# An encoder layer with 32 experts on one core: the block between the experts' weight products in another order

## The chip, the cores and the metric

One core of one Trainium2 chip runs the whole layer in one launch. The metric is the device time of the launch in microseconds (us), median of several runs. The kernel before takes 993.62 us (3 runs, 993.09 to 994.04).

## What is computed

The layer has three parts on 512 tokens of 1024 channels: a mixer (convolution and dilated attention), a cross-attention into 256 memory rows, and a mixture of 32 SwiGLU experts of width 512 with two experts per token; a last RMSNorm follows. The change lies in the experts and the last norm:

```
gates = p_g[:, None] * softmax(top_v)                # two experts per token
y_rows = (silu(xb @ w1[e]) * (xb @ w3[e])) @ w2[e]   # for the tokens of expert e
y = segment_sum(y_rows * row_gate, row_tok)          # back to the tokens
out = rms_norm(x + y, final_norm_g)
```

Every expert's weights (6.29 MB in float32) are read once: 201 MB in all.

## The kernel before

Each expert has 64 slots; two experts are a pair, whose 2 x 64 slots fill the 128 rows of a tile. `RK` holds for each token and expert the rank of the token in the expert (0 if it isn't there), `RT` is its transpose in bf16, experts on the partitions. `experts` (L1213) runs eight **rounds** d = 0 to 7 of four experts (two pairs):

- **Products.** `experts_up` multiplies the gathered tokens `xT` by w1 and w3 of the four experts of round d (PSUM banks "pj" for the first pair, "s" for the second). From round 1 on, `experts_down` then multiplies the hidden rows of round d-1, `eT`, by w2 (banks "tr","tr" for the first pair, "o","m" for the second) and `gated` scales the result by the slots' gates: ScalarE writes the high part of `ys`, VectorE the low part.
- **The block between.** `hidden_turned` turns the new hidden rows (8 transposes, "pj"). `hot` writes the one-hot matrix `onehot` of the next four experts (VectorE), `gather4` gathers their tokens by 64 matmuls of 128x256 (`onehot` against the rows `hm`; banks "s","s","pj","pj"), and `put` copies them to `xT`. `one_hots` makes `ct`, the transposed one-hots of round d-1's experts: for each of the four experts a matmul that spreads one row of `RT` over 128 partitions of a "tr" bank, and a compare on VectorE of 64 of these partitions with the slot number. `slot_gates` computes the gates of the next slots (8 matmuls of 128x8 into "o" and "m", read by ScalarE and VectorE). `scatter` adds the outputs to the tokens: 8 tiles of four matmuls 128x512 (`ct` against `ys`; banks "tr","o","tr","m"), each followed by an add to `xacc` on VectorE (L1211).

Round 0 has no down products and no scatter, round 7 no gather. Behind the loop stand the last round's two pairs: pair 14 (`one_hots`, `experts_down`, `scatter`) and pair 15 (`experts_last`: three groups of columns, each with its product, `gated` and `scatter`, and the last norm's steps between). `finish_begin` (L1279) prepares the last norm: it spreads `final_norm_g` over 128 partitions, `fg`, with eight VectorE products, eight matmuls (L1292, 16 in the trace) and two ScalarE copies (L1293); `fg` is first read by GpSimd at L1305, behind the scatter of the first group.

TensorE's instructions inside the rounds are kept in the order in which the code is written; the other engines' order is set when the program is built, by a scheduler.

**Weights.** They come in pieces of 512 KB, 48 in a full round, over SyncE's queue, into a ring of 29 regions in SBUF. A piece is issued when the products have read the region's former content (`load` at the end of each step of the products), at most eight are under way, and they are issued in the order of use. So the transfers run ahead of the products by up to 29 pieces.

Of the kernel before, what the change touches and what calls it, by code (L numbers as in the profile page):

```python
# [12 lines left out]
AF = mybir.ActivationFunctionType  # L13
ALU = mybir.AluOpType
# [4 lines left out]
D = 1024  # L19
# [8 lines left out]
NE = 32  # L28
# [9 lines left out]
V_XA, V_MEM, V_MOE, V_DW, V_DB, V_LG, V_LB, V_CO, V_AO, V_FN, V_MIX, V_N = 0, 8, 16, 24, 86, 88, 90, 92, 94, 100, 108, 116  # L38
# [31 lines left out]
def rows(ap, n):  # L70

    return bass.AP(tensor=ap.tensor, offset=ap.offset, ap=[[0, 128], [1, n]])
# [12 lines left out]
class K:  # L85
# [984 lines left out]
            return oh, x, rest  # L1070
        return add, end

    def gather4(self, d, oh, xT):

        for b, tag in enumerate(("s", "s", "pj", "pj")):
            p = self.ps(tag)
            for cc in (2 * b, 2 * b + 1):
                for t in range(NT):
                    self.take(p, oh, cc, t, t == 0, t == NT - 1)
            for cc in (2 * b, 2 * b + 1):  # L1080
                self.put(xT, p, cc)
# [28 lines left out]
                self.nc.vector.tensor_tensor(gt[q, j:j + 1], gt[q, j:j + 1], p[q, 4 + e:5 + e], op=ALU.add)  # L1110
        return gt

    def one_hots(self, pr, ct):

        for i in range(2):
            p = self.ps("tr")
            e = 2 * pr + i
            self.mm(p, self.idb[:, e:e + 1].to_broadcast([128, 128]), self.RT, start=True, stop=True)
            q = slice(i * 64, i * 64 + 64)
            self.nc.vector.tensor_scalar(ct[q, :], p[q, :], self.slot[q, :], None, op0=ALU.is_equal)  # L1120

    def experts_up(self, d, xT, rest=None):

# [34 lines left out]
    def hidden(self, j):  # L1158
        return self.eT[:, j, :].rearrange("p (a b) -> p a b", a=4)

    def experts_down(self, pr, gt):

        j = pr % 2
        hT = self.hidden(j)
        ps = [self.ps(tag) for tag in (("tr", "tr"), ("o", "m"))[j]]
        for k in range(4):
            w = [self.piece(pr, 2, k, e) for e in range(2)]
            for h in range(2):
                for i in range(2):
                    self.mm(ps[h][i * 64:i * 64 + 64, :], hT[:, k, i * 64:i * 64 + 64], w[i][:, h, :],  # L1170
                            start=k == 0, stop=k == 3)
            self.load(2)
        out = []
        for h in range(2):
            ys = self.wsp.tile([128, 2, 512], F32R, name="ys", tag="wlo")
            self.gated(ys, ps[h], gt, 512)
            out.append(ys)
        return out
# [34 lines left out]
    def experts(self, oh, xT, rest):  # L1213


        self.sl = self.eT = None
        with self.in_order():
            gt, ys = None, []
            for d in range(NE // 4):
                self.experts_up(d, xT, rest if d == 0 else None)  # L1220
                last = d == NE // 4 - 1
                if d == 0:
                    now = self.slot_gates(0, oh)
                if d:
                    ys = [self.experts_down(2 * d - 2 + j, gt[:, j:j + 1]) for j in range(2)]
                gt = now
                self.hidden_turned()
                if not last:
                    for t in range(NT):
                        self.hot(oh, d + 1, t)  # L1230
                    self.gather4(d + 1, oh, xT)
                if d:
                    ct = self.wsp.tile([128, 2, 512], F32R, name="ct", tag="whi")
                    for j in range(2):
                        self.one_hots(2 * d - 2 + j, ct[:, j, :])
                if not last:
                    now = self.slot_gates(d + 1, oh)
                if d:
                    for h in range(2):
                        self.scatter([(ct[:, j, :], ys[j][h]) for j in range(2)], h * 512, 512, ("tr", "o", "tr", "m"))  # L1240
                    ys = ct = None
            xT = None
            ct = self.wsp.tile([128, 2, 512], F32R, name="ct", tag="whi")
            for j in range(2):
                self.one_hots(NE // 2 - 2 + j, ct[:, j, :])
            y = self.experts_down(NE // 2 - 2, gt[:, 0:1])
            for h in range(2):
                self.scatter([(ct[:, 0, :], y[h])], h * 512, 512, ("tr", "o", "tr", "m"))
        self.experts_last(NE // 2 - 1, self.hidden(1), ct[:, 1, :], gt[:, 1:2])
# [29 lines left out]
    def finish_begin(self):  # L1279

        nc = self.nc
        r = [self.region(PIECES.index((NE // 2 - 3, 2, k, e))) for k in range(4) for e in range(2)]
        flat = [v.rearrange("p a b -> p (a b)") for v in r[0:6]]
        self.fg, dg, self.fo = flat[0], flat[1], flat[2:6]
        self.fj, self.fk = r[6][:, 0, :], r[6][:, 1, :]
        for i in range(2):
            p = self.ps("pj")
            for c in range(4):
                d = dg[:, i * 512 + c * 128:i * 512 + c * 128 + 128]
                v = V_FN + i * 4 + c  # L1290
                nc.vector.tensor_scalar(d, self.ident, self.VT[:, v:v + 1], None, op0=ALU.mult)
                nc.tensor.matmul(p[:, c * 128:c * 128 + 128], self.ones, d, start=True, stop=True)  # L1292
            nc.scalar.activation(self.fg[:, i * 512:i * 512 + 512], p, AF.Copy)  # L1293
        self.fss = self.xm.tile([128, NT, 3], F32, name="fss")
        self.frs = self.sm.tile([128, NT], F32, name="frs", bufs=1)

# [284 lines left out]
```

## Time and profile before

| what | value |
|---|---|
| median of 3 runs | 993.62 us |
| the profiled execution's own time | 992.92 us |
| its span, first to last instruction | 991.1 us |
| TensorE matmul busy | 954.9 us (96%) |
| VectorE busy | 465.6 us (47%) |
| ScalarE busy | 304.3 us (31%) |
| HBM read | 239.96 MB |

The profile's times are us from the start of the span. A matmul's end is modelled, so durations of neighbouring matmuls overlap; the distance from one start to the next is what counts. A float32 product of 128x512 appears as two instructions. The granted clock is a share of 2.4 GHz: 1.00 is 2.4 GHz, 0.50 is 1.2 GHz.

### The profile page before, as it was taken

Reading aid. Unit: us, or ns where it says so; the run is one execution under the profiler, and the core shown is the slowest. Engines: PE = TensorE matmul, PEld = TensorE weight load, DVE = VectorE, ACT = ScalarE, POOL = GpSimd, SP = SyncE. Lnnn points to the kernel's source line nnn. Section 1 sums busy time; section 2 is a strip of 40 time slices with the busy share of each in tenths; the row PEclk is TensorE's granted clock in tenths of the full one; section 3 lists DMA queues with packets and bytes.
Section 4 is the critical chain, followed back from the end, with each engine's and each line's share of the span. In section 5 each row is a group of like instructions: output and inputs, shape, how many; then the busy total and the mean of one; then the engine's idle time right before and its main releaser. Section 6 shows DMA issues by size and latency. Waiting matters only on the chain.

```text
span 991.1 us, 15255 instructions
## 1 busy us (share of the span) xinstructions
PE 954.9 (96%) x5804; PEld 652.3 (66%) x5804; DVE 465.6 (47%) x1110; ACT 304.3 (31%) x683; POOL 202.0 (20%) x245
## 2 busy tenths in 40 slices
PE   8999999999999999999999899899899999999994
PEld 7988788878899988999363543735436345364352
DVE  6679777777756455547220420502414124032256
ACT  7525565656534445435110200101011010020113
POOL 3159998973310001101000000000000000000002
PEclk9999999999999999999999989899998998999997
DMA  6421201222364126653889999999999999999932
GB/s 214 135 80 48 81 29 38 64 87 85 120 219 142 44 86 234 255 191 128 324 326 397 409 341 409 409 353 409 382 409 409 377 409 364 400 409 400 404 104 87
DMA packets 102744, 243.10 MB, mean 245 GB/s; under 512 B 11288, under 2 KB 51596, under 8 KB 102668
## 3 DMA queue, kind: packets, MB, share of 16 engines
q1 hardware_dynamic: 102668, 242.09, 65.2%
q8 instruction: 47, 0.77, 0.3%
q14 instruction: 29, 0.24, 0.1%
HBM read 239.96 MB, written 2.10 MB: 244 GB/s over the span
## 4 chain that ended last, share of the span: by engine, by line
PE 89%; DVE 6%; POOL 2%; issue 1%; DMA 1%; SPq 0%; ACT 0%; DVEq 0%; POOLq 0%; ACTq 0%
PE ps_pj L147 36%; PE ps_s L147 21%; PE ps_tr L147 9%; PE ps_o L147 6%; PE ps_m L147 6%; PE ps_o L587 2%; PE ps_tr L573 2%; PE ps_s L552 2%; DVE ct L1120 1%; PE ps_s L551 1%; PE ps_pj L151 1%; POOL sg L424 1%; DVE onehot L1027 1%; PE ps_tr L151 1%; DVE xacc L1211 1%
## 5 line engine op out<-in xcount | busy, mean ns | idle before, releaser
L147 PE MATMUL ps_pj<-ring,xT 128*64 128x512 f32 x504 | 111.8, 594 | 0.3 <-DVE xT L1043 0.3
L147 PE MATMUL ps_s<-ring,xT 128*64 128x512 f32 x496 | 107.8, 592 | 0.0
L1305 POOL TENSOR_TENSOR ring<-xacc,ring 128x512 f32<-128x512 f32 x4 | 5.0, 1284 | 503.0 <-DVE xacc L1211 503.0
L115 DVE TENSOR_TENSOR wlo<-wst,whi 128x512 fp32r<-128x512 f32 x104 | 79.7, 797 | 30.2 <-ACT whi L114 29.7
L147 PEld LDWEIGHTS ps_s<-ring,xT 128*64 128x64 f32 x496 | 35.6, 137 | 70.8 <-issue 65.9
L147 PEld LDWEIGHTS ps_pj<-ring,xT 128*64 128x64 f32 x504 | 36.0, 137 | 70.1 <-issue 66.7
L114 ACT ACTIVATE whi<-wst 128x512 fp32r<-128x512 f32 x108 | 62.4, 625 | 47.8 <-PE ps_pj L147 14.0
L147 PE MATMUL ps_pj<-whi,hT_hi 128*128 128x256 f32 x256 | 74.9, 293 | 0.3 <-DVE rv L502 0.3
L147 PE MATMUL ps_pj<-wlo,hT_hi 128*128 128x256 f32 x256 | 74.5, 292 | 0.0
L147 PE MATMUL ps_pj<-whi,hT_lo 128*128 128x256 f32 x256 | 73.6, 288 | 0.0
L147 PE MATMUL ps_tr<-ring,eT 128*64 128x512 f32 x256 | 56.5, 593 | 0.0
L1145 DVE TENSOR_TENSOR sl<-sl,ps_s 128x512 f32<-128x512 f32 x8 | 5.5, 688 | 103.9 <-PE ps_s L147 103.9
L1145 DVE TENSOR_TENSOR sl<-sl,ps_pj 128x512 f32<-128x512 f32 x8 | 5.5, 689 | 102.8 <-PE ps_pj L147 92.1
L147 PEld LDWEIGHTS ps_pj<-whi,hT_hi 128*128 128x128 f32 x256 | 48.8, 191 | 4.3 <-issue 3.1
L147 PEld LDWEIGHTS ps_pj<-wlo,hT_hi 128*128 128x128 f32 x256 | 48.8, 191 | 2.4 <-issue 2.2
L147 PEld LDWEIGHTS ps_pj<-whi,hT_lo 128*128 128x128 f32 x256 | 48.9, 191 | 1.7 <-issue 1.7
L1144 ACT ACTIVATE sl<-ps_pj 128x512 f32<-128x512 f32 x8 | 4.8, 597 | 146.8 <-PE ps_pj L147 146.8
L560 ACT ACTIVATE pw<-pw,nm 128x512 f32<-128x512 f32 x48 | 34.5, 719 | 31.6 <-DVE nm L558 28.0
L147 PEld LDWEIGHTS ps_tr<-ring,eT 128*64 128x64 f32 x256 | 18.3, 137 | 36.2 <-issue 36.0
L424 POOL TENSOR_TENSOR sg<-sg,ctmp 128x512 f32<-128x512 f32 x30 | 41.4, 1378 | 1.3
L563 POOL TENSOR_SCALAR pw<-pw,rd 128x512 f32<-128x512 f32 x48 | 37.1, 775 | 21.3 <-DVE rd L562 14.2
L147 PE MATMUL ps_tr<-ys,ct 128*128 128x512 f32 x120 | 40.2, 460 | 0.5 <-DVE ct L1120 0.5
(386 smaller groups left out, 2134.7 us busy)
## 6 DMA issues: line engine op xcount, KB each, us to landing
ring<-in_w_dram SPq DMA_DIRECT2D x374, 512.0 KB
wst<-in_w_in_dram SPq DMA_DIRECT2D x24, 256.0 KB
wst<-in_w_in_dram SPq DMA_DIRECT2D x10, 512.0 KB
wst<-in_w_xk_dram SPq DMA_DIRECT2D x8, 512.0 KB
wst<-in_w_xv_dram SPq DMA_DIRECT2D x8, 512.0 KB
wst<-in_w_out_dram SPq DMA_DIRECT2D x8, 512.0 KB
wst<-in_w_xq_dram SPq DMA_DIRECT2D x8, 512.0 KB
wst<-in_w_xo_dram SPq DMA_DIRECT2D x8, 512.0 KB
```

Source lines behind the costliest of these rows:

```text
L114: nc.scalar.activation(hi, src, AF.Copy)
L115: (eng or nc.vector).tensor_tensor(lo, src, hi.bitcast(F32), op=ALU.subtract)
L147: ins = self.nc.tensor.matmul(*args, **kw)
L151: ins = self.nc.tensor.transpose(out, in_, self.ident)
L424: nc.gpsimd.tensor_tensor(self.cacc[:, 0, :], self.cacc[:, 0, :], tmp, op=ALU.add)
L551: nc.tensor.matmul(p, q, kh, start=True, stop=False)
L552: nc.tensor.matmul(p, q[own, :], kl[own, :], start=False, stop=True)
L560: nc.scalar.activation(w, w, AF.Exp, bias=nm, scale=0.125, accum_out=den)
L563: nc.gpsimd.tensor_scalar(w, w, rd, 1.0, op0=ALU.mult, op1=ALU.mult)
L573: self.nc.tensor.transpose(p2[:, kt * 128:kt * 128 + 128], ws[t][:, kt * 128:kt * 128 + 128], self.ident)
L587: nc.tensor.matmul(o[i * 64:i * 64 + 64, half * 256:half * 256 + 256], v[kt][:, vo + i * 64:vo + i * 64 + 64], pts[i][half][:, kt, :], sta ...
L1145: nc.vector.tensor_tensor(sl, sl, hs[1], op=ALU.mult)
```

## The change

`ranks_spread` is new: it spreads the ranks of two experts into one bank, 64 partitions each, so that `one_hots` compares 128 partitions at once (two compares a round and not four). The spreads stand right behind the down products, the compares ahead of the gather on VectorE, the gates between the two halves of the gather. Behind the loop, pair 14's spreads stand ahead of its product, which now goes into the banks "s","s". `final_norm_g` comes to 128 partitions by one DMA.

```diff
-    def gather4(self, d, oh, xT):
+    def gather4(self, d, oh, xT, tags):
-        for b, tag in enumerate(("s", "s", "pj", "pj")):
+        for b, tag in tags:
...
-    def one_hots(self, pr, ct):
+    def ranks_spread(self, pr):
+        p = self.ps("tr")
         for i in range(2):
-            p = self.ps("tr")
             e = 2 * pr + i
-            self.mm(p, self.idb[:, e:e + 1].to_broadcast([128, 128]), self.RT, start=True, stop=True)
-            q = slice(i * 64, i * 64 + 64)
-            self.nc.vector.tensor_scalar(ct[q, :], p[q, :], self.slot[q, :], None, op0=ALU.is_equal)
+            self.mm(p[i * 64:i * 64 + 64, :], self.idb[:, e:e + 1].to_broadcast([128, 64]), self.RT, start=True, stop=True)
+        return p
+
+    def one_hots(self, p, ct):
+        self.nc.vector.tensor_scalar(ct, p, self.slot, None, op0=ALU.is_equal)
...
-                if d:
-                    ys = [self.experts_down(2 * d - 2 + j, gt[:, j:j + 1]) for j in range(2)]
-                gt = now
-                self.hidden_turned()
                 if not last:
                     for t in range(NT):
                         self.hot(oh, d + 1, t)
-                    self.gather4(d + 1, oh, xT)
+                if d:
+                    ys = [self.experts_down(2 * d - 2 + j, gt[:, j:j + 1]) for j in range(2)]
+                    spread = [self.ranks_spread(2 * d - 2 + j) for j in range(2)]
+                gt = now
+                self.hidden_turned()
                 if d:
                     ct = self.wsp.tile([128, 2, 512], F32R, name="ct", tag="whi")
                     for j in range(2):
-                        self.one_hots(2 * d - 2 + j, ct[:, j, :])
+                        self.one_hots(spread[j], ct[:, j, :])
                 if not last:
+                    self.gather4(d + 1, oh, xT, ((0, "s"), (1, "s")))
                     now = self.slot_gates(d + 1, oh)
+                    self.gather4(d + 1, oh, xT, ((2, "pj"), (3, "pj")))
...
+            spread = [self.ranks_spread(NE // 2 - 2 + j) for j in range(2)]
+            y = self.experts_down(NE // 2 - 2, gt[:, 0:1], ("s", "s"))
             ct = self.wsp.tile([128, 2, 512], F32R, name="ct", tag="whi")
             for j in range(2):
-                self.one_hots(NE // 2 - 2 + j, ct[:, j, :])
-            y = self.experts_down(NE // 2 - 2, gt[:, 0:1])
+                self.one_hots(spread[j], ct[:, j, :])
...
-        for i in range(2):
-            p = self.ps("pj")
-            for c in range(4):
-                ...
-                nc.vector.tensor_scalar(d, self.ident, self.VT[:, v:v + 1], None, op0=ALU.mult)
-                nc.tensor.matmul(p[:, c * 128:c * 128 + 128], self.ones, d, start=True, stop=True)
-            nc.scalar.activation(self.fg[:, i * 512:i * 512 + 512], p, AF.Copy)
+        nc.sync.dma_start(self.fg, rows(self.a["final_norm_g"], D))
```

How the instructions move. TensorE in the block of a middle round, before (`ps_tr<-rkT,idb` is a spread, `early,sl` the transposes, `onehot,hm` the gather, `ghl,onehot` the gates, `ys,ct` the scatter; the spread stands four times in a row):

```order
L151 MATMUL ps_pj<-early,sl 128x128 x8
L147 MATMUL ps_s<-onehot,hm 128x256 x32
L147 MATMUL ps_pj<-onehot,hm 128x256 x32
L147 LDWEIGHTS idb
L147 MATMUL ps_tr<-rkT,idb 128x512
...
L147 MATMUL ps_o<-ghl,onehot 128x8 x4
L147 MATMUL ps_m<-ghl,onehot 128x8 x4
L147 MATMUL ps_tr<-ys,ct 128x512 x4
```

The same place in the changed kernel:

```order
L147 LDWEIGHTS idb
L147 MATMUL ps_tr<-rkT,idb 64x512
...
L151 MATMUL ps_pj<-early,sl 128x128 x8
L147 MATMUL ps_s<-onehot,hm 128x256 x32
L147 MATMUL ps_o<-ghl,onehot 128x8 x4
L147 MATMUL ps_m<-ghl,onehot 128x8 x4
L147 MATMUL ps_pj<-onehot,hm 128x256 x32
L147 MATMUL ps_tr<-ys,ct 128x512 x4
```

The spreads went from between gather and scatter to ahead of the transposes, and the gates from just ahead of the scatter to the middle of the gather; nothing but gather matmuls stands ahead of the scatter now.

VectorE in the same block of the changed kernel (`ys` is the gating, `ct` the compare, `xT` the copy of gathered tokens, `gt` the gates, L1027 the one-hots of the round after next):

```order
L1188 SCALAR_TENSOR_TENSOR ys<-ps_m,gt,ys 128x512
L108 COPY eT<-ps_pj 128x512
L1123 TENSOR_SCALAR ct<-ps_tr,early 128x512 x2
L1043 TENSOR_SCALAR xT<-ps_s,gmo 128x256 x2
L1110 TENSOR_TENSOR gt<-gt,ps_o 64x1
L1110 TENSOR_TENSOR gt<-gt,ps_m 64x1
...
L1043 TENSOR_SCALAR xT<-ps_pj,gmo 128x256 x2
L1027 TENSOR_TENSOR onehot<-iota,RK 128x256 x4
L1214 TENSOR_TENSOR xacc<-xacc,ps_tr 128x512
```

The compares are ahead of every copy of the gather. The four one-hots L1027 stand whole ahead of the first add of the scatter.

TensorE behind the loop, from the last tile of round 7's scatter, before (`ring,eT` into "tr" is pair 14's product, into "s" pair 15's):

```order
L147 MATMUL ps_tr<-rkT,idb 128x512
L147 MATMUL ps_s<-ring,eT 64x512 x2
...
L147 MATMUL ps_tr<-ring,eT 64x512 x14
L147 MATMUL ps_s<-ring,eT 64x512 x2
L147 MATMUL ps_s<-ring,eT 64x256 x8
L147 MATMUL ps_tr<-ys,ct 128x512 x2
L147 MATMUL ps_o<-ys,ct 128x512 x2
```

The same place in the changed kernel:

```order
L147 MATMUL ps_tr<-rkT,idb 64x512
L147 MATMUL ps_s<-ring,eT 64x512 x16
L147 MATMUL ps_tr<-ys,ct 128x512 x2
L147 MATMUL ps_o<-ys,ct 128x512 x2
...
L147 MATMUL ps_s<-ring,eT 64x512 x8
L147 MATMUL ps_s<-ring,eT 64x256 x8
L147 MATMUL ps_o<-y_8733,ct 128x512 x2
```

Pair 15's first product was spread between pair 14's spreads and product; now it stands behind pair 14's whole scatter.

## Rows read from the trace of the kernel before

**Rows 1.** The page: the engines' busy time (us, share of the span, instructions), and what the DMA engines moved in each of 40 slices of 24.8 us, in GB/s.

```profile
PE 954.9 (96%) x5804; PEld 652.3 (66%) x5804; DVE 465.6 (47%) x1110; ACT 304.3 (31%) x683; POOL 202.0 (20%) x245
...
GB/s 214 135 80 48 81 29 38 64 87 85 120 219 142 44 86 234 255 191 128 324 326 397 409 341 409 409 353 409 382 409 409 377 409 364 400 409 400 404 104 87
```

**Rows 2.** The table of windows by stage: the products of rounds 2 to 7 (from the start of the first up product to the end of the last down product), and of the blocks between, those of rounds 1 and 3. The other blocks lie between the products' rows. Columns: window, its length and TensorE's busy time with instructions, weight loads, VectorE, ScalarE, GpSimd; TensorE's granted clock; DMA share; GB/s.

```profile
554.90:579.10 24.20, 21.32 (x118) 17.70 (x116) 13.45 (x26) 3.55 (x11) 0.00 (x0) 0.86 1.02 407
579.10:620.50 41.40, 41.40 (x194) 13.77 (x193) 3.60 (x6) 3.25 (x5) 0.00 (x0) 1.00 0.95 370
...
644.30:685.70 41.40, 41.40 (x194) 13.74 (x193) 3.58 (x6) 3.25 (x5) 0.00 (x0) 1.00 0.96 376
685.70:707.00 21.30, 18.42 (x120) 15.61 (x118) 13.43 (x26) 3.55 (x10) 0.00 (x0) 1.00 1.02 408
707.00:748.40 41.40, 41.40 (x194) 13.77 (x194) 3.62 (x6) 3.25 (x5) 0.00 (x0) 1.00 1.00 394
...
771.50:812.90 41.40, 41.40 (x194) 13.76 (x194) 3.62 (x6) 3.25 (x5) 0.00 (x0) 1.00 0.99 390
...
836.10:877.50 41.40, 41.40 (x194) 13.75 (x193) 3.59 (x6) 3.25 (x5) 0.00 (x0) 1.00 0.97 376
...
898.30:939.60 41.30, 41.30 (x193) 13.66 (x192) 5.13 (x13) 3.25 (x5) 0.00 (x0) 1.00 1.02 402
```

**Rows 3.** The chain of work that ended last, in order of time, in the block of round 1. Columns: start, length, what.

```profile
563.96 0.74 DVE ct L1120
...
567.09 0.76 DVE onehot L1027 x2
...
569.39 0.24 DVE gt L1110 x2
...
569.70 2.04 PE ps_o L147 x4
571.74 1.71 PE ps_tr L147 x4
...
578.27 0.91 PE ps_m L147 x4
```

**Rows 4.** The timeline of the same block, TensorE (PE) and its weight loads (PEld). Columns: start, length, engine, line, operation, out<-in, shapes, count, and in brackets the idle time before and what ended it.

```profile
554.93 0.86 PEld L151 LDWEIGHTS ps_pj<-early,sl 128*128 128x128 f32 x8 [0.81 <-issue]
...
555.76 3.89 PEld L147 LDWEIGHTS ps_s<-onehot,hm 128*128 128x128 f32 x32
...
559.58 3.91 PEld L147 LDWEIGHTS ps_pj<-onehot,hm 128*128 128x128 f32 x32
...
563.54 0.60 PE L147 MATMUL ps_tr<-rkT,idb 128*128 128x512 bf16 x2
...
565.55 0.63 PEld L147 LDWEIGHTS ps_o<-ghl,onehot 128*128 128x128 f32 x4 [0.69 <-issue]
...
566.54 0.30 PEld L147 LDWEIGHTS ps_tr<-ys,ct 128*128 128x128 f32 x2
```

**Rows 5.** The table of windows for the first part of round 1's scatter (columns as in rows 2).

```profile
569.70:575.20 5.50, 5.50 (x13) 4.35 (x14) 1.38 (x3) 0.00 (x0) 0.00 (x0) 0.50 1.02 407
```

**Rows 6.** The waits of SyncE's queue from 522 to 912 us: who waited for whom, us in total, times, longest.

```profile
SPq L1005 <- PE ps_pj L147: 70.1, 43, 8.9
```

**Rows 7.** The table of windows of 5 us at the end of the weights' transfers (columns as in rows 2).

```profile
925.00:930.00 5.00, 5.00 (x26) 1.65 (x24) 0.69 (x1) 0.00 (x0) 0.00 (x0) 1.00 1.02 406
930.00:935.00 5.00, 5.00 (x26) 1.72 (x24) 2.17 (x6) 1.37 (x2) 0.00 (x0) 1.00 1.03 410
935.00:940.00 5.00, 5.00 (x26) 1.69 (x23) 1.28 (x6) 0.96 (x2) 0.00 (x0) 1.00 1.03 394
940.00:945.00 5.00, 4.49 (x30) 3.00 (x28) 4.62 (x7) 2.15 (x4) 0.00 (x0) 1.00 1.07 370
945.00:950.00 5.00, 5.00 (x22) 4.15 (x23) 3.43 (x5) 0.00 (x0) 0.00 (x0) 1.00 0.82 258
950.00:955.00 5.00, 5.00 (x21) 2.02 (x19) 4.22 (x7) 0.00 (x0) 0.00 (x0) 1.00 0.00 0
```

**Rows 8.** The timeline from the last down product of round 7 to the last norm (columns as in rows 4): the last two pieces' products, the transposes, the second tile of round 7's scatter, pair 14's first spread, the gating of pair 14, pair 15's first scatter tile, the first use of `fg`, the first step of the last norm.

```profile
937.79 1.03 PE L147 MATMUL ps_o<-ring,eT 128*64 128x512 f32 x4
...
939.61 1.09 PE L151 MATMUL ps_pj<-early,sl 128*128 128x128 f32 x8
...
945.47 1.09 PE L147 MATMUL ps_o<-ys,ct 128*128 128x512 f32 x4
...
951.84 0.61 PE L147 MATMUL ps_tr<-rkT,idb 128*128 128x512 bf16 x2
...
962.23 1.52 ACT L1182 ACTIVATE ys<-ps_tr,gt 128x512 fp32r<-128x512 f32 x2 [18.53 <-PE ps_tr L147]
...
971.66 0.70 PE L147 MATMUL ps_o<-y,ct 128*128 128x512 f32 x2
...
973.44 5.01 POOL L1305 TENSOR_TENSOR ring<-xacc,ring 128x512 f32<-128x512 f32 x4 [502.96 <-DVE xacc L1211]
...
977.49 1.24 DVE L1312 CUSTOM_DVE_ANT_0 ring<-xacc 128x256 f32<-128x256 f32 x1
```

**Rows 9.** The groups of instructions by line and shape from 440 us on: us busy, mean ns of one, idle time before.

```profile
L1185 DVE SCALAR_TENSOR_TENSOR ys<-ps_tr,gt,ys 128x512 fp32r<-128x512 f32 x16 | 12.0, 751 | 49.6 <-ACT ys L1182 48.8
L1211 DVE TENSOR_TENSOR xacc<-xacc,ps_tr 128x512 f32<-128x512 f32 x34 | 23.2, 684 | 12.1 <-PE ps_tr L147 12.1
```

More of the change, by code (lines that the diff above doesn't have):

```diff
@@ L1159, in hidden, with experts_down @@
         return self.eT[:, j, :].rearrange("p (a b) -> p a b", a=4)
-    def experts_down(self, pr, gt):
+    def experts_down(self, pr, gt, tags=None):
         j = pr % 2
         hT = self.hidden(j)
-        ps = [self.ps(tag) for tag in (("tr", "tr"), ("o", "m"))[j]]
+        ps = [self.ps(tag) for tag in tags or (("tr", "tr"), ("o", "m"))[j]]
         for k in range(4):
@@ L1240, in experts @@
                         self.scatter([(ct[:, j, :], ys[j][h]) for j in range(2)], h * 512, 512, ("tr", "o", "tr", "m"))
-                    ys = ct = None
+                    ys = ct = spread = None
             xT = None
+            spread = [self.ranks_spread(NE // 2 - 2 + j) for j in range(2)]
+            y = self.experts_down(NE // 2 - 2, gt[:, 0:1], ("s", "s"))
             ct = self.wsp.tile([128, 2, 512], F32R, name="ct", tag="whi")
             for j in range(2):
-                self.one_hots(NE // 2 - 2 + j, ct[:, j, :])
-            y = self.experts_down(NE // 2 - 2, gt[:, 0:1])
+                self.one_hots(spread[j], ct[:, j, :])
             for h in range(2):
@@ L1282, in finish_begin @@
         r = [self.region(PIECES.index((NE // 2 - 3, 2, k, e))) for k in range(4) for e in range(2)]
-        flat = [v.rearrange("p a b -> p (a b)") for v in r[0:6]]
-        self.fg, dg, self.fo = flat[0], flat[1], flat[2:6]
+        flat = [v.rearrange("p a b -> p (a b)") for v in r[0:5]]
+        self.fg, self.fo = flat[0], flat[1:5]
         self.fj, self.fk = r[6][:, 0, :], r[6][:, 1, :]
-        for i in range(2):
-            p = self.ps("pj")
-            for c in range(4):
-                d = dg[:, i * 512 + c * 128:i * 512 + c * 128 + 128]
-                v = V_FN + i * 4 + c
-                nc.vector.tensor_scalar(d, self.ident, self.VT[:, v:v + 1], None, op0=ALU.mult)
-                nc.tensor.matmul(p[:, c * 128:c * 128 + 128], self.ones, d, start=True, stop=True)
-            nc.scalar.activation(self.fg[:, i * 512:i * 512 + 512], p, AF.Copy)
+        nc.sync.dma_start(self.fg, rows(self.a["final_norm_g"], D))
         self.fss = self.xm.tile([128, NT, 3], F32, name="fss")
```

## The prediction, made before the changed kernel was timed

> **What bounds the kernel now.** I read the page first. TensorE's matmuls are busy for 96% of the span, and in the second half of the span the DMA engines move 409 GB/s in eight slices and clearly less in others [rows 1]. So two things lie close together there, and the average doesn't tell which one ends last. The table of windows by stage does [rows 2]. In the products of each round TensorE is busy without a gap (41.40 of 41.40 us) at the full clock, and no product waits for weights. The reader is to see the last column too: in the block of round 1 the DMA engines run at 407 GB/s, but in the products that follow at 370, and at 376, 394, 390, 376 and 402 in the later ones. The transfers stop for a while behind every block: the ring is full, and SyncE's queue waits for TensorE to read a region, up to 8.9 us at a time [rows 6]. Hence TensorE sets the pace and the transfers follow.
>
> What is lost, is lost in the block. The chain of waits in round 1's block [rows 3] goes from the gather through VectorE: the compares `ct` from 563.96 on, then the one-hots, then the gates at 569.39, and at 569.70 the scatter's second tile, which needs the bank that the gates had. Then comes a second loss. Four scatter matmuls take 1.71 us at 571.74 and 0.91 us at 578.27: after six thin microseconds the granted clock is 0.50, the lower level of 1.2 GHz [rows 5]. Round 3's block had the same waits but kept the clock at 1.00, and is 21.3 us long against 24.2 [rows 2]. So of 24.2 us some 3 us are the clock's.
>
> **The rounds, TensorE alone.** The new block costs, from starts in round 1's timeline [rows 4]: four spreads; two followed each other inside 0.60 us, so 0.22 us each, 0.9 in all (half of that if the two 64-column halves of a bank run side by side, which no spread in the trace shows). Transposes 0.83 (554.93 to 555.76). Gather 3.82 and 3.96 (to 563.54). Gates 0.99 (565.55 to 566.54). Scatter 8 tiles at 0.91 [rows 3], 7.3. Sum 17.8 us.
>
> Does anything wait in it? The compares: VectorE has `ys`, the `eT` copy and two compares ahead of it, about 4 x 0.75 us from the end of the down products, and the scatter comes only 10.5 us after that end. I price the compare of 128 partitions like that of 64 (0.74 us [rows 3]), the nearest row. The spread's "tr" banks were read during the second pair's product. The gates get their banks before the first half of the gather ends, and hand "o" and "m" back in its second half, 4 us ahead of the scatter. The four one-hots (0.76 for two [rows 3]) now stand ahead of the first add: that add starts some 1.9 us after the gather's end, the first tile's bank is wanted again at 4 x 0.91 = 3.6 us, and an add takes 0.68 [rows 9], so 1 us is left. All covered; if that cover failed, each bank would come back a microsecond late, twice a round. Lower bound of the block 17.3, upper bound the block with the lower clock, 17.8 + 3 = 20.8.
>
> The blocks of rounds 1 to 6 were 24.2, 23.8, 21.3, 23.1, 23.2 and 20.8 us (the distances in [rows 2]), 136.4 together. At 17.8 they take 106.8: **29.6 us** less for TensorE, and a round 41.4 + 17.8 = 59.2 us.
>
> **The rounds, the weights.** A round reads 48 pieces of 512 KB, 25.17 MB: at 409 GB/s [rows 1] 61.5 us. That is more than 59.2. So a faster block finds the transfers behind it, and what can be gained is what they lose now. First, their stops: (409 - 370)/409 x 41.4 = 3.9 us in round 2, then 3.3, 1.5, 1.9, 3.3 and 0.7 [rows 2], together 14.8 us. With a block that ends 6 us earlier the first region comes free before the ring is full, so I take all of it. Second, their lead at the end of round 7's products: all has landed by 950, and 16 pieces (8.39 MB) follow the last piece of these products; 930 to 950 moved 7.16 MB, the other 1.23 MB took 3.0 us before [rows 7], so that piece landed at 927.0. It is used at 937.8 [rows 8]: 10.8 us of lead. Sum 14.8 + 10.8 = **25.6 us**, by which the products of round 7 can end earlier. It is below 29.6, so it decides: the lead shrinks by some 2 us a round, and in rounds 5 to 7 the last products wait for pieces. Only if the blocks averaged over 18.5 us would TensorE decide again.
>
> **Behind the products of round 7.** Before, the second scatter tile starts at 945.47, 5.9 us after the transposes [rows 8]: four compares and two bank changes stand ahead. Now the spread is over at 0.9 and both compares at 2.4; I put that tile at 3.0: 2.9 us gained. From pair 14's first spread to its gating it was 10.4 us (951.84 to 962.23 [rows 8]), with spreads, waits and part of pair 15's product between; now 0.9 for the spreads and 32 product records at half of 0.43 us, 6.9: gating starts after 7.6, 2.8 gained. The part moved away comes back: pair 14's scatter must wait for its gating (0.75 for the low part [rows 9]), its tiles run at the adds' pace, and only then come pair 15's products (3.4 and 1.9 us). Pair 15's first scatter tile was 9.4 us behind the gating (971.66), and will be about 11; the last norm's first step was 15.3 behind it (977.49 [rows 8]) and will be 17.7: 2.4 lost. Net 3.3 us, with bounds of 0 and 6.
>
> `fg`: what is removed lay inside the 5.9 us above, so nothing beyond them. The new DMA moves 512 KB, as much as a piece, so 1.3 us at 409 GB/s. It is the last in SyncE's queue ahead of the output and delays no weights. It lands near 937 (950 - 14.8 and a little), and GpSimd wants it when the first adds of pair 15 are done, some 29 us before 973.44 [rows 8]: 7 us later. Cost nothing.
>
> **Sum.** 25.6 + 3.3 = 28.9 us from the profiled execution's 992.92 gives 964.0; its time is 0.7 below the median, so 964.7 for the median. Round 0's block keeps its instructions and its length.
>
> **Rivals.**
> 1. *The clock still falls in the blocks.* In round 1 the fall came behind the waits, but round 3 had the same waits without it, so the rows don't show exactly what brings it. If each block loses 3 us, it takes 20.8: TensorE decides again, 136.4 - 124.8 = 11.6, with the tail 14.9: 978.7. Against it: no row has the low clock in a stretch of products or gather without waits. 0.12.
> 2. *The weights don't bind*, because the transfers reach more than 409 GB/s or I misread the lead. Then TensorE's 29.6 and the tail's 3.3 count, 960.7; with the 17.3 us block 957.7. No slice of [rows 1] is above 409. 0.08.
> 3. *Waiting for pieces lowers the clock.* In the late rounds two pieces are read in 1.72 us and land in 2.57 us, so TensorE idles a third of the time. If the clock then falls, two pieces take 3.44 us, and the last rounds fall behind the transfers. A fall lasts some 7 us in round 1 (569.7 to 576 [rows 3]), and costs up to 3.5 us if nothing later absorbs it; two such, 971.7. The Trainium skill ("TensorE: Matmul & The Clock Gate", section "HAM oscillation — how this bites in real kernels") speaks for this rival: short stretches of matmuls between waits for a DMA let the clock fall in the wait, so that the next stretch starts slow. The trace before has no product that waits for a DMA long enough to try that; its one agreeing row is the fall behind the waits on VectorE [rows 5], its one disagreeing row round 3 [rows 2]. 0.12.
> 4. *`fg` comes late* and the kernel ends slower. Its 128 rows are read from one and the same 4 KB. To eat 28.9 us and 2 more it must land 31 us after GpSimd wants it, about 975, so some 40 us for 512 KB: 13 GB/s, against 258 GB/s in the thinnest row of the weights' end [rows 7]. No row shows such a read. 0.03.
> 5. *A wait inside the block that I called covered* (the adds behind the one-hots, or a bank of the gates) keeps 1 to 3 us a block: TensorE decides, 968 to 980. The order of the instructions shows that the change does move what it says, so it doesn't simply do nothing. 0.07, of which 0.02 for no gain that can be told.
>
> **How the numbers follow.** The forecast, weights binding, has 0.58, with a range of its own from 961 to 969 (tail 0 to 6, lead and rate 1 us). A measurement here can tell 0.2%, 2 us, from no change. The range 959 to 974 takes in the forecast, rival 3, most of rival 2 and part of rival 5; it leaves out rivals 1 and 4. Faster 0.95, same 0.02, slower 0.03.
>
> **What would show it.** Right: blocks of about 17.8 us between products from round 1 to 6, no wait on `ct` or `gt`, granted clock 1.00 in the blocks; DMA at 409 GB/s without a dip from 522 us to the end; waits of weight loads for the ring in rounds 5 to 7; the weights' end near 935. Wrong: dips in GB/s that remain, clocks of 0.5 in the scatter, waits for the ring before round 4, or a tail from the end of round 7's products that isn't 3 us shorter.

## The result, and the profile after

The changed kernel takes 965.76 us (median of 4 runs, 964.75 to 967.0) beside 993.83 for the kernel before on the same chip: a ratio of 0.9718, with a 95% interval of 0.9702 to 0.9735. The forecast was 964.7, in a range from 959 to 974. The profiled execution took 967.0 us, the longest of the four; its span is 965.2 us. One of the six runs of `two_wide_alone` below was in a slower state (1064.71 us, at a mean granted clock of 0.845) and is in none of the figures.

The page of after: busy times, the chain's shares by engine and by line, and GB/s in slices of 24.1 us.

```profile
PE 942.1 (98%) x5788; PEld 645.7 (67%) x5788; DVE 450.6 (47%) x1086; ACT 301.8 (31%) x681; POOL 201.7 (21%) x245
...
GB/s 219 134 88 44 46 66 26 64 88 110 75 220 154 47 87 89 231 380 43 202 400 318 409 409 409 409 409 408 409 408 409 409 410 408 410 409 409 409 334 89
...
PE 74%; DMA 19%; DVE 3%; POOL 2%; issue 1%; ACT 1%; SPq 0%; DVEq 0%; POOLq 0%; ACTq 0%
PE ps_pj L147 32%; DMA ring<-in_w_dram 18%; PE ps_s L147 16%; PE ps_tr L147 5%; PE ps_o L147 4%; PE ps_m L147 4%; PE ps_o L587 2%; PE ps_tr L573 2%; PE ps_s L552 2%; PE ps_s L551 1%; POOL sg L424 1%; PE ps_tr L151 1%; DMA wst<-in_w_in_dram 1%; PE ps_pj L151 1%; DVE sg L430 1%
```

Against [rows 1] the dips have gone: from 530 us to the end of the weights every slice moves 408 to 410 GB/s. And the transfers of the ring now stand in the chain of work with 18% of the span. The busy share of TensorE alone (98%) would have hidden that.

The table of windows by stage, as in [rows 2]: the products of round 1, the block of round 1, the products of round 2, and then those of rounds 5, 6 and 7.

```profile
516.30:557.70 41.40, 41.40 (x195) 13.91 (x196) 3.75 (x8) 4.09 (x7) 0.00 (x0) 1.00 0.93 359
...
557.70:575.00 17.30, 17.30 (x118) 15.40 (x116) 11.73 (x24) 3.29 (x10) 0.00 (x0) 1.00 1.03 409
575.00:616.30 41.30, 41.30 (x194) 13.85 (x196) 3.60 (x6) 3.25 (x5) 0.00 (x0) 1.00 1.03 409
...
750.90:795.20 44.30, 43.68 (x195) 14.35 (x195) 3.57 (x5) 3.18 (x5) 0.00 (x0) 1.00 1.03 409
...
812.60:857.70 45.10, 44.29 (x196) 14.35 (x196) 3.57 (x5) 3.23 (x5) 0.00 (x0) 1.00 1.03 409
...
875.10:919.10 44.00, 43.55 (x195) 14.58 (x195) 3.57 (x5) 3.19 (x5) 0.00 (x0) 1.00 1.03 409
```

Round 1's block is 17.3 us where it was 24.2, at the clock 1.00 where it was 0.86. All six blocks measure 17.3 within 0.1. The products keep 41.3 up to round 4; those of rounds 5, 6 and 7 take 44.3, 45.1 and 44.1 by their first and last starts, so 9.6 us more than 3 x 41.3. SyncE's queue, over the stretch of [rows 6], waits for TensorE little:

```profile
SPq L1005 <- PE ps_pj L147: 11.1, 23, 2.4
```

The chain in round 1's block (start, length, what) answers to [rows 3] and [rows 4]:

```profile
557.69 0.43 PE ps_tr L147 x4
558.12 1.03 PE ps_pj L151 x8
559.15 3.83 PE ps_s L147 x32
562.98 0.34 PE ps_o L147 x4
563.32 0.45 PE ps_m L147 x4
563.77 3.94 PE ps_pj L147 x32
567.71 0.93 PE ps_tr L147 x4
568.64 0.91 PE ps_o L147 x4
...
574.08 0.91 PE ps_m L147 x4
```

TensorE is followed by TensorE all through: no `ct`, no `onehot` and no `gt`, and each scatter tile takes 0.91 (the first 0.93). The sum can be read off: 0.43 + 1.03 + 3.83 + 0.79 + 3.94 + 7.28 = 17.30.

### The profile page after: what moved, and what is told of

Read it like the earlier page. It is cut to its first block, busy times and chain, and to the rows that moved or that the text cites. A ratio compares the mean times of both kernels' runs of the same rounds, so it can differ in the third digit from the quotient of the medians.

```text
span 965.2 us, 15189 instructions
## 1 busy us (share of the span) xinstructions
PE 942.1 (98%) x5788; PEld 645.7 (67%) x5788; DVE 450.6 (47%) x1086; ACT 301.8 (31%) x681; POOL 201.7 (21%) x245
## 4 chain that ended last, share of the span: by engine, by line
PE 74%; DMA 19%; DVE 3%; POOL 2%; issue 1%; ACT 1%; SPq 0%; DVEq 0%; POOLq 0%; ACTq 0%
PE ps_pj L147 32%; DMA ring<-in_w_dram 18%; PE ps_s L147 16%; PE ps_tr L147 5%; PE ps_o L147 4%; PE ps_m L147 4%; PE ps_o L587 2%; PE ps_tr L573 2%; PE ps_s L552 2%; PE ps_s L551 1%; POOL sg L424 1%; PE ps_tr L151 1%; DMA wst<-in_w_in_dram 1%; PE ps_pj L151 1%; DVE sg L430 1%
## 5 line engine op out<-in xcount | busy, mean ns | idle before, releaser
L147 PE MATMUL ps_tr<-ring,eT 128*64 128x512 f32 x224 | 49.7, 592 | 0.0
L560 ACT ACTIVATE pw<-pw,nm 128x512 f32<-128x512 f32 x48 | 34.5, 719 | 32.5 <-DVE nm L558 28.9
L147 PE MATMUL ps_o<-ring,eT 128*64 128x512 f32 x112 | 40.7, 602 | 1.9 <-DMA ring<-in_w_dram 1.8
L424 POOL TENSOR_TENSOR sg<-sg,ctmp 128x512 f32<-128x512 f32 x30 | 41.3, 1377 | 1.2
L147 PE MATMUL ps_m<-ring,eT 128*64 128x512 f32 x112 | 38.6, 597 | 0.0
```

Source lines behind the costliest of these rows:

```text
L147: ins = self.nc.tensor.matmul(*args, **kw)
L424: nc.gpsimd.tensor_tensor(self.cacc[:, 0, :], self.cacc[:, 0, :], tmp, op=ALU.add)
L560: nc.scalar.activation(w, w, AF.Exp, bias=nm, scale=0.125, accum_out=den)
```

## The experiments

**One part alone.** `two_wide_alone` is the kernel before with spreads and compares two experts wide, in the old place; `gates_mid_alone` is the kernel before with the gates between the halves of the gather.

```diff
 # two_wide_alone, in one_hots
+        p = self.ps("tr")
...
-            p = self.ps("tr")
...
-            self.mm(p, self.idb[:, e:e + 1].to_broadcast([128, 128]), self.RT, ...)
+            self.mm(p[i * 64:i * 64 + 64, :], self.idb[:, e:e + 1].to_broadcast([128, 64]), self.RT, ...)
...
+        self.nc.vector.tensor_scalar(ct, p, self.slot, None, op0=ALU.is_equal)
 # gates_mid_alone
-                    self.gather4(d + 1, oh, xT)
+                    self.gather4(d + 1, oh, xT, ((0, "s"), (1, "s")))
+                    now = self.slot_gates(d + 1, oh)
+                    self.gather4(d + 1, oh, xT, ((2, "pj"), (3, "pj")))
...
-                if not last:
-                    now = self.slot_gates(d + 1, oh)
```

> The kernel before with one part of the change alone: two experts' ranks in one bank and two compares for four, in the old place between gather and scatter, gates and tail as before. Theory (the weights bind only when the blocks average under 18.5 us): the compares end 1.5 us earlier, so the gates, and the scatter behind them, come 1.5 to 1.7 us earlier in six blocks, and about 2 us are gained behind the loop: 12 us less, 981 to 982, TensorE still sets the pace and the transfers still stop; if the shorter wait also keeps the clock at 2.4 GHz, up to 12 us more, 970. Rival (the compares alone are the gain, the order adds nothing): 966, and products that wait for weights.

> The kernel before with another part alone: the gates between the two halves of the gather, the four spreads and four compares as before. Theory: the scatter no longer waits for the gates, but on VectorE the four one-hots of the next round (1.4 us) now stand ahead of the four compares, which end about 5 us behind the gather; the block is some 21.4 us at the full clock and 24 with the fall, so 0 to 12 us less, 982 to 994. Rival (the wait for the gates' banks was the cost): 6 x 3 us less, 976 or below.

`two_wide_alone` took 974.8 us (five runs), ratio 0.9805 (0.9786 to 0.9825), between its two cases; `gates_mid_alone` 981.21, ratio 0.9872 (0.9854 to 0.989), a little better than its range. Their rivals, 966 and 976 or below, are out. TensorE's waits for VectorE (total, times, longest), first of the kernel before from 500 to 950 us, then of `two_wide_alone` and of `gates_mid_alone` from 500 to 940:

```profile
PE ps_o L147 <- DVE gt L1110: 8.1, 5, 1.9
PE ps_tr L147 <- DVE ct L1120: 6.6, 13, 0.6
```

```profile
PE ps_o L147 <- DVE gt L1110: 8.0, 5, 1.6
PE ps_tr L147 <- DVE ct L1119: 0.9, 1, 0.9
```

```profile
PE ps_tr L147 <- DVE ct L1120: 11.0, 19, 1.0
```

Each part removes its own wait, all but one of 0.9 us, and the other one stays or, for the compares, grows. The blocks are 17.8 to 21.0 us with two-wide spreads and 20.2 to 22.2 with the gates amid the gather. The clock fell in two blocks of the one and in one of the other, for 3.4 us each, where the kernel before has it in five of six, mostly for 6.8. So with less waiting there were fewer falls, and in the blocks of the whole change there is none. What exactly makes it fall is not settled: round 3 of before had the same waits and no fall [rows 2].

**Work stuffed into a block.** If the weights decide in the late rounds, time added to early blocks must cost nothing, and time added to the last one all but the late waits behind it.

```diff
-            for cc in (2 * b, 2 * b + 1):
+            for cc in (2 * b, 2 * b + 1) * (2 if b in twice else 1):
 # stuffed_early: twice = (0,) in rounds 1 to 4;  stuffed_late: (0, 1) and (2, 3) in round 6
```

> The changed kernel with 16 gather matmuls done twice (1.9 us of TensorE's time, the same result) in the blocks of rounds 1 to 4, 7.7 us in all. Theory (in the late rounds TensorE waits for weights, about 9.7 us in all by its trace): the time stays within 1 us of the changed kernel's 965.8, and the late waits shrink from 9.7 to 2 us. Rival (TensorE sets the pace all through): 7.7 us more, 973.5.

> The changed kernel with the whole gather done twice in the block of round 6 alone, 64 matmuls, the same 7.7 us. Theory: behind that block only round 7's waits are left to take it up, 2.8 us, so 4.9 us more than the changed kernel, 970.7. Rival (TensorE sets the pace): 7.7 us more, 973.5. Rival (the weights' last transfer alone sets the end): nothing more, 965.8.

`stuffed_early`: 966.59, ratio 0.9718 (0.9705 to 0.9732), the change's own, although four blocks grew to 19.3 us: the late waits shrank from 9.6 to 2.5 us instead. `stuffed_late`: 970.33, ratio 0.9761 (0.9747 to 0.9774), with a last block of 25.1 us and round 7's products at 41.3. Both as the theory has it. This decides against rival 2: TensorE does not set the end of the rounds.

**Fewer pieces, and pieces in other places.** `change_again` is the changed kernel once more. `four_pieces_less` and `pieces_24_less` leave out the transfer of 4 and of 24 pieces (their products read what lies in the ring, so the outputs are other numbers). `three_more_slots` loads the first three `w2` pieces of round 1 into slots beside the ring in round 0's block, when the transfers would stop.

```diff
 # four_pieces_less, pieces_24_less, in load
-            if left > 4:
+            if PIECES[n] in SKIP:
+                pass
+            elif left > 4:
...
 # three_more_slots, in experts_down, at the end and in experts
-            self.load(2)
+            self.load(sum(PIECES.index((pr, 2, k, e)) not in FIRST for e in range(2)))
...
-FIRST = (15, 28, 29, 30, 31, 32)
+FIRST = (15, 28, 29, 30, 31, 32, 64, 65, 66)
...
+                    for i in (6, 7, 8):
+                        self.load_first(i)
```

> The changed kernel once more, beside the runs that are compared with it. All theories: 964 to 968, ratio 0.970 to 0.974 to the kernel before.

> The changed kernel without the transfer of four pieces (half of w3 of one pair in round 4; the products read what the ring held before, so these experts' outputs are other numbers). Theory (weights bind in the late rounds): 4 x 1.28 = 5.1 us less than the changed kernel, 960.7, late waits 4.6 us in place of 9.7. Rival (TensorE sets the pace): no difference, 965.8.

> The changed kernel without 24 pieces (all of w3 of one pair in each of rounds 4 to 6, outputs of these experts other numbers), 30.7 us of transfers. Theory: the transfers fall out of the bound altogether and TensorE alone decides; its waits of 9.7 us go and nothing more, 956, blocks and products unchanged (17.3 and 41.4 us). Rival (the transfers are the only bound): 30 us less, 935.

> The changed kernel, with the first three down pieces of round 1 taken out of the ring and loaded into three tiles of the weights' first slots, which are idle from the end of round 0's up products until round 1's gating. Theory: the transfers' one remaining stop, behind round 0, gets three more pieces to move, 3.8 us, and as the transfers bind to the end, all of that comes off: 962. Rival (TensorE sets the pace, or the stop is no loss): 965.8.

Measured in this order, on one chip: 965.84 (0.9715, 0.9696 to 0.9733), 960.51 (0.9654, 0.9637 to 0.9671), 956.25 (0.9615, 0.96 to 0.9631) and 962.64 (0.9681, 0.9665 to 0.9696). Four pieces are 2.1 MB, 5.1 us at 409 GB/s, and saved 5.3, with late waits of 4.7 us; with 24 less all products take 41.3 us and the kernel gains 9.6, just what the late waits were: then TensorE decides. The slots beside the ring keep the transfers going where the change still stops. The windows of 515 to 530 us, first of after, then of `three_more_slots`:

```profile
515.00:520.00 5.00, 5.00 (x30) 2.48 (x30) 1.77 (x5) 0.84 (x2) 0.00 (x0) 1.00 0.40 130
520.00:525.00 5.00, 5.00 (x26) 1.67 (x24) 0.00 (x0) 0.00 (x0) 0.00 (x0) 1.00 0.87 294
525.00:530.00 5.00, 5.00 (x26) 1.63 (x24) 0.00 (x0) 0.60 (x1) 0.00 (x0) 1.00 0.95 365
```

```profile
515.00:520.00 5.00, 5.00 (x28) 2.17 (x28) 1.43 (x4) 0.84 (x2) 0.00 (x0) 1.00 1.02 401
520.00:525.00 5.00, 5.00 (x26) 1.70 (x24) 0.00 (x0) 0.00 (x0) 0.00 (x0) 1.00 0.93 318
525.00:530.00 5.00, 5.00 (x26) 1.60 (x24) 0.09 (x1) 0.60 (x1) 0.00 (x0) 1.00 1.02 409
```

401 - 130, 318 - 294 and 409 - 365 GB/s over 5 us each are 1.70 MB, about the three pieces (1.57 MB, 3.8 us at 409). It saved 3.2, so 0.6 of the 3.8 didn't come. That version beats both kernels, and computes all that they do.

**The norm's vector and the end.** `old_norm_vector` is the change with `fg` made by products and matmuls as before. `tail_products_first` puts the first group of pair 15's products ahead of pair 14's scatter, so that TensorE needn't wait for the adds; `slots_and_tail` has this and the three slots. `old_order_of_pair_14` gives pair 14 its old order.

```diff
 # old_norm_vector
-        nc.sync.dma_start(self.fg, rows(self.a["final_norm_g"], D))
...
+                nc.vector.tensor_scalar(d, self.ident, self.VT[:, v:v + 1], None, op0=ALU.mult)
+                nc.tensor.matmul(p[:, c * 128:c * 128 + 128], self.ones, d, ...)
...
 # tail_products_first, in experts and experts_last
-            y = self.experts_down(NE // 2 - 2, gt[:, 0:1], ("s", "s"))
+            y = self.experts_down(NE // 2 - 2, gt[:, 0:1], ("o", "m"))
...
-                self.scatter([(ct[:, 0, :], y[h])], h * 512, 512, ("tr", "o", "tr", "m"))
...
             first = out(0)
+            self.scatter([(ct0, y0[0])], 0, 512, ("tr", "pj"))
             todo = out(1)
+            self.scatter([(ct0, y0[1])], 512, 512, ("tr", "pj"))
 # old_order_of_pair_14
-            spread = [self.ranks_spread(NE // 2 - 2 + j) for j in range(2)]
-            y = self.experts_down(NE // 2 - 2, gt[:, 0:1], ("s", "s"))
...
-                self.one_hots(spread[j], ct[:, j, :])
+                self.one_hots(self.ranks_spread(NE // 2 - 2 + j), ct[:, j, :])
+            y = self.experts_down(NE // 2 - 2, gt[:, 0:1])
```

> The changed kernel with final_norm_g spread as before, by eight VectorE products, sixteen matmul instructions and two ScalarE copies in place of the DMA. Theory (that part lies beside other work either way): within 1.5 us of the changed kernel's 965.8; the matmuls now stand inside round 7's scatter, so if anything up to 1 us more. Rival (the DMA is worth the change's tail): 2 us or more above.

> The changed kernel with the end in another order: pair 14's product in the banks o and m, pair 15's first product right behind it and ahead of pair 14's scatter, whose tiles take the banks tr and pj, pair 15's second product amid it. Theory (in the tail TensorE and VectorE wait for each other: pair 15's first product, 3.4 us, stands behind pair 14's whole scatter, and VectorE idles 2.75 us for it): 1 to 2 us less, 964 to 965. Rival (the adds and gatings on VectorE alone set the tail): the adds start 2.5 us later and the time is 965.8 or up to 2 more.

> The three more slots and the other tail together. Theory (the weights set when the products end, the tail is a chain of its own, so both add): the three slots' 962.6 less 1 to 2 us, 961. Rival (they share a limit): 962.6 or above.

> The changed kernel with one thing put back behind the loop: pair 14's two spreads stand each with its compare again, as the kernel before has the order, and its product takes the banks tr again. The spreads stay two experts wide, the rounds and the norm's vector as changed. In the changed kernel the stretch from the end of round 7's products to the end took 46.1 us, 5.4 less than before, where I had forecast 3.3: 2.9 by the second scatter tile of round 7, and 2.8 - 2.4 = 0.4 by the new order of pair 14. Theory: the terms measured in the trace (pair 14's gating 3.7 earlier behind its spreads, 2.1 lost behind the gating) make the new order worth about 1.6 us, so this kernel takes 967.4 with a last stretch of 47.7 us. First rival: the 0.4 was right and the rest comes from the norm's vector, which this kernel keeps: 966.2, last stretch 46.5. Second rival: the old order takes back the whole excess and more, as pair 15's first products then stand ahead of pair 14's again: 968.5 or above, last stretch 49. Blocks of 17.4 us and late waits for weights as in the changed kernel by all three.

`old_norm_vector`: 968.51, ratio 0.9732 (0.9716 to 0.9747). Its stretch behind round 7's products is 49.3 us in the one profile, against 46.1 and 46.2 in the two of the change; but the ratio says only 1.5 us, and its interval overlaps the change's. By its time, 2.7 us above 965.8, the expectation's rival would hold, by the ratio its theory, so it decides neither. The scheduler also moved pair 15's products amid pair 14's scatter in it, so the edit isn't clean. That `fg` cost something before is likely, not shown.

`tail_products_first`: 967.36, ratio 0.9722 (0.9708 to 0.9735), no gain, so the expectation fell and its rival's number held. VectorE's timeline, first pair 15's gating in the change, then the adds of pair 14 in `tail_products_first`:

```profile
944.92 0.75 DVE L1188 SCALAR_TENSOR_TENSOR y<-ps_s,gt,y 128x512 fp32r<-128x512 f32 x1 [2.75 <-ACT y L1185]
```

```profile
937.89 0.69 DVE L1214 TENSOR_TENSOR xacc<-xacc,ps_tr 128x512 f32<-128x512 f32 x1 [2.61 <-PE ps_tr L147]
...
941.81 0.69 DVE L1214 TENSOR_TENSOR xacc<-xacc,ps_tr 128x512 f32<-128x512 f32 x1 [0.78 <-PE ps_tr L147]
...
943.92 0.69 DVE L1214 TENSOR_TENSOR xacc<-xacc,ps_pj 128x512 f32<-128x512 f32 x1 [1.02 <-PE ps_pj L147]
```

In the change VectorE gates pair 14's output, adds eight times without a pause and then stands idle for 2.75 us, until pair 15's product is there. Here it stands idle for 2.61 us ahead of the adds and again at each product that was put between. So the idle time was moved and not removed: counted from the end of round 7's products, the adds begin 2.7 us later and the end comes 1.3 us later. That VectorE alone sets the pace there is not shown. `slots_and_tail`: 963.84, ratio 0.9687 (0.9673 to 0.97), the three slots' own gain, where 961 was expected.

`old_order_of_pair_14`: its last stretch is 47.7 us, as the theory had it, but the time 967.09, ratio 0.9719 (0.9705 to 0.9732), cannot be told from the change's 0.9718 and 0.9715. The 1.6 us of the profile are below what its runs resolve, and they don't tell the theory (967.4) from the first rival (966.2).

## Why the prediction was right, and where its terms were off

**The block**: forecast 17.8, measured 17.3, its lower bound. The 0.5 is the spread: I took 0.22 us for each of four and named half of that as possible. It is what happened, four in 0.43 (the chain at 557.69): the two 64-column halves run side by side. The transposes took 0.2 more than I had and the gates 0.2 less. None of the waits that I called covered appeared. TensorE's waits from 500 to 950 us:

```profile
PE ps_o L147 <- DMA ring<-in_w_dram: 1.8, 9, 0.2
PE ps_tr L147 <- DVE ys L1188: 0.3, 1, 0.3
```

The one wait for VectorE is that of pair 14's scatter for its gating, behind the loop, so rival 5 is out.

**The clock**: rival 1 (0.12) did not come; 1.00 in every block. Rival 3 (0.12) had its condition and not its effect. TensorE did wait for pieces as foreseen. In the timeline of round 6's last products (start, length, and in brackets the idle time by modelled ends) and the windows around them:

```profile
850.01 0.59 PE L147 MATMUL ps_o<-ring,eT 128*64 128x512 f32 x1
850.81 0.64 PE L147 MATMUL ps_o<-ring,eT 128*64 128x512 f32 x1 [0.20 <-DMA ring<-in_w_dram]
```

```profile
845.00:850.00 5.00, 4.79 (x21) 1.48 (x18) 1.50 (x2) 1.37 (x2) 0.00 (x0) 1.00 1.03 410
850.00:855.00 5.00, 4.60 (x18) 1.33 (x16) 0.00 (x0) 0.00 (x0) 0.00 (x0) 1.00 1.02 404
```

From one start to the next it is 0.80 us where an undisturbed pair of products shows about 0.43, and 18 matmuls stand in 5 us where [rows 7] has 26; yet the granted clock stays 1.00, 2.4 GHz. The bracket's 0.20 is only what is left beyond the modelled end, so the starts tell the wait and the busy share hides it. The Trainium skill ("TensorE: Matmul & The Clock Gate", section "HAM oscillation — how this bites in real kernels") has the clock falling in waits for a DMA that are longer than the matmuls between them. Here they are half as long, some 0.4 us beside 0.86, and the rule didn't show. The rival stretched it to a case that the section doesn't describe. What longer waits in the products would do, no run here shows.

**The weights**: that they decide was right, shown by the stuffed blocks and the fewer pieces, and they ran at 409 GB/s. The size was off. From round 1's first product to the end of round 7's it was 425.94 us (513.58 to 939.52) and is 402.87 (516.27 to 919.14): 23.1 gained, not 25.6. The term that was off is the lead of 10.8 us, which I took from bytes: the last piece "landed at 927.0". The chain of after shows when that piece comes (start, length, what):

```profile
907.15 10.18 DMA ring<-in_w_dram
917.32 0.04 issue
917.37 0.64 PE ps_o L147
```

And the windows show the bytes behind it:

```profile
915.00:920.00 5.00, 4.79 (x21) 1.50 (x18) 0.80 (x2) 1.35 (x2) 0.00 (x0) 1.00 1.03 412
920.00:925.00 5.00, 5.00 (x25) 3.84 (x24) 4.56 (x8) 0.62 (x2) 0.00 (x0) 1.00 1.02 404
925.00:930.00 5.00, 5.00 (x26) 3.23 (x26) 4.12 (x7) 0.00 (x0) 0.00 (x0) 1.00 1.04 386
930.00:935.00 5.00, 5.00 (x26) 1.68 (x24) 0.50 (x1) 0.00 (x0) 0.00 (x0) 1.00 1.03 344
935.00:940.00 5.00, 4.71 (x21) 2.60 (x16) 4.10 (x7) 1.37 (x2) 0.00 (x0) 1.00 0.66 230
```

From 915 on 8.88 MB move; without `fg` (0.52) that is 8.36, almost the 8.39 MB of 16 pieces. So by bytes the piece was there at 914.9, and by the chain it landed 2.4 us later: 25.6 - 2.4 = 23.2, beside the 23.1 measured.

The traces show why. Eight transfers are under way, one takes 10.18 us from issue to landing, 8 x 1.28, and each lands in sixteen parts, with a mark in the trace for every part. Those of this piece landed from 913.52 to 917.32, and the first part of the next piece already at 914.80. So the bytes counted up to 914.9 hold parts of later pieces, and some of this one are missing. Before the change the parts of the same piece landed from 926.89 to 928.74, 1.7 us behind the count of 927.0, so the lead was really 9.1 us. By bytes the stops' 14.8 were gained in full, and from 530 to 917 us no slice is below 408; by landings they gave 14.1, and 14.1 + 9.1 is 23.2 again. The last piece landed at 939, where I had the weights' end near 935: the windows above fall below 400 GB/s from 925 on.

**The end**: forecast 3.3 of 0 to 6, measured 51.5 - 46.1 = 5.4. The timeline of after, against [rows 8]:

```profile
919.66 1.09 PE L151 MATMUL ps_pj<-early,sl 128*128 128x128 f32 x8
...
921.95 1.07 PE L147 MATMUL ps_o<-ys,ct 128*128 128x512 f32 x4
...
928.39 0.62 PE L147 MATMUL ps_tr<-rkT,idb 128*64 128x512 bf16 x4
...
928.84 7.03 PE L147 MATMUL ps_s<-ring,eT 128*64 128x512 f32 x32
...
933.92 0.42 SPq L1292 DMA_DIRECT2D ring<-in_final_norm_g_dram  x1
...
935.10 1.52 ACT L1185 ACTIVATE ys<-ps_s,gt 128x512 fp32r<-128x512 f32 x2 [14.09 <-PE ps_s L147]
...
945.81 0.73 PE L147 MATMUL ps_o<-y,ct 128*128 128x512 f32 x2
...
947.35 5.03 POOL L1304 TENSOR_TENSOR ring<-xacc,ring 128x512 f32<-128x512 f32 x4 [474.28 <-DVE xacc L1214]
...
952.45 0.42 DVE L1311 CUSTOM_DVE_ANT_0 ring<-xacc 128x256 f32<-128x256 f32 x1
```

The second scatter tile comes 2.85 us behind the products' end, where it was 6.0 (forecast 3.0). From pair 14's spread to its gating it is 6.7 for 10.4: 3.7 gained, 0.9 more than my 2.8. My sum was wrong there: 0.9 + 6.9 is 7.8 and not 7.6. Measured are 0.45 for the spreads and 6.26 from the product's start to the gating, which begins when the first of the product's two banks is done, ahead of the last of the 32 records. From the gating to the last norm's first step it is 17.35 for 15.3: 2.1 lost (2.4). The way from there to the end, 12.75 for 13.6, gave 0.85 that I didn't have. `fg` is issued at 933.92, its last part landed at 940.2, and GpSimd's first use at 947.35 waits for an add: hidden, with 7 us to spare, and rival 4 is out.

**The sum**: 23.1 + 5.4 = 28.5 in the profiles where 28.9 stood: 2.5 too much for the weights, 2.1 too little for the end. That the sum comes so near is luck, as the two errors cancel. The profiled execution of after reached round 1's products 2.7 us later than that of before, in a part that the change doesn't touch (in the experiments that leave that part alone it ended between 514.5 and 517.0), so the medians, 28.1 apart, are the better measure.

## What to carry to other kernels

When a stage is made faster, ask first which resource had slack behind it and how much of it is usable: here 32.6 us came off the blocks (136.4 - 6 x 17.3), the transfers let the products end 23.1 earlier, and the rest turned into waits for weights, where stretching four blocks by 1.9 us each then cost nothing. A lead counted in bytes is too long where parts of later transfers are in the count; take the landing of the very piece that is used. And the next gain then lies with the new bound (a stop of the transfers far ahead of it, at 515 us), not with the stage that has just been improved.

## What the hardware showed that was not expected

- Two bf16 matmuls of 64 columns by 512 into the two halves of one bank run side by side: a group of four shows 0.62 us (928.39 in the timeline above), where two of 128 columns show 0.60 [rows 4].
- A compare of 128 partitions takes 0.74 us, as long as one of 64 (0.74 [rows 3]; 0.75 in the median of the 32 before).
- Waits of some 0.4 us for weights behind every 0.86 us of products left TensorE at 2.4 GHz, although 18 products stood in 5 us and not 26.
- Eight transfers of 512 KB under way take 10.18 us each and keep 409 GB/s; the sixteen parts of one land up to 3.8 us apart (913.52 to 917.32), the last 2.4 us behind the byte count.
